# A decoder trunk on one core: first norm's squares on VectorE, more places for split weights and score blocks

## The chip, the cores and the metric

The kernel runs on one core of a Trainium2 chip. The core has TensorE (PE, matrix products; a row "PEld" is its weight load), VectorE (DVE), ScalarE (ACT) and GpSimd (POOL), which run side by side, each in the order of its own instruction list, and SyncE (SP), which issues most DMA transfers. SBUF is the on-chip memory that the engines work in, PSUM the banks that PE adds into, DRAM the chip's large memory. The metric is the time of one execution on the device in microseconds, less is better. An instruction starts when those ahead of it in its engine's list have started and the data and places that it needs are there.

## What is computed

Two decoder layers on 1024 tokens of width 1024, float32. Layer 0 mixes tokens by retention heads and RWKV-7 heads, layer 1 by attention over a window of 128 tokens with a learned sink for each head; each is followed by a dense SwiGLU network.

```python
for layer in range(2):
    n = rms_norm(h, norm1_g[layer])
    h = h + (retention_rwkv_mixer(n, ...) if layer == 0 else swa_sink_mixer(n, ...))
    n = rms_norm(h, norm2_g[layer])
    h = h + (silu(n @ w_gate) * (n @ w_up)) @ w_down
return rms_norm(h, final_g)

# swa_sink_mixer, a block of 128 queries against 256 keys
s = where(valid, q @ k.T / 8, -inf)
m = maximum(s.max(-1), sink)
e = exp(s - m)
o = (e / (e.sum(-1) + exp(sink - m))) @ v
```

## The kernel before

Activations lie transposed, 128 channels on the partitions and tokens along the row, in two halves of 512 tokens (hf 0 and 1). A float32 product is made of three products in a faster type: every operand is split into a high part (a cast on ACT) and a low part (value minus high part), and `gemm` (L327) adds hi x hi, hi x lo and lo x hi for each of eight blocks of 128 channels, 24 matmuls of 128x512 for one column of weights.

**Split weights.** `wraw` (L288) loads a raw column into one of two "wr" places. `wsplit` (L310) casts it in two pieces on ACT (L318) and subtracts on POOL (L319), into tiles from `wtile` (L305): a ring of four "w" places, two for a column, or, while `w6` is set, of six that take in the two "wr" places too. In layer 0's input projection the first half's split columns are also written to DRAM (`keep`, L321), and the second half loads them back with `wkept` (L295). `Plan` (L105) orders that layer when the program is built: it holds the projection columns as jobs (`prefetch`, L135, loads the next two), and advances generators such as `first_norm` (L495) by due times. After that the tile framework's scheduler sets the final order of each engine's list from its own model of time, so an edit moves more than the lines it touches.

**First norm.** `loads` (L471) issues x and the first two weight columns. `first_norm` multiplies each of eight blocks of x by the norm's gain and splits it (`gained`, L444, L449 on ACT and L450 on DVE), squares it on ACT (L505), and has PE sum each square over the channels by a product with a matrix of ones: eight products into one PSUM tile. `factor` (L455) then takes the logarithm (L459) and the exponential (L460) for the inverse root rs, and POOL multiplies it into the rotary cos and sin (L464). The evacuation of a projection multiplies by rs, so PE starts with projections before rs is known. rs also goes into `second_norm` for the second half.

**Around the second layer** (from L1690 on): `down` and `rest_d` (L1447) finish layer 0's network, `rest_d(0)` for the first half, `rest_d(1)` for the second; a column of the latter is split ahead. `attn` (L1472) does the first half's attention while two columns' worth and more of `rest_d(1)` remain as fill; `form0` (L1103) normalises the first half for the next network, block by block: product with the norm (`normed`, L1099, on DVE into one of four "u0" places), a write to DRAM, and `split` (L337), whose cast is on ACT (L339) and whose low part (L341) alternates between POOL and DVE. `ffn_early` (L1216) does first products of the network. In layer 1 `form0` and the early columns stand beside the second half's attention.

**Attention.** For each of four groups of heads two q columns are projected (`proj`, L1479, evacuation L1483 and L1484), then four blocks of 128 queries follow: scores on PE (L1526), mask added on DVE into a tile "s" (L1530), maximum on DVE (L1536), exponentials on ACT (L1543), scaling on DVE (L1549), transposes on PE (L1556) into PSUM, copies into "pT" (L1558 on ACT, L1560 on DVE), products with v on PE (L1566), split of the result (L1572 on ACT, L1573 on DVE). There are two "s" places, three of the small "st4" and two "pT", and the tiles that hold v before its transposes (L1507) use the "s" places as well.

## Time and profile before

| | us |
|---|---|
| median of 3 runs | 2442.09 (2437.88 to 2443.95) |
| profiled execution, its own time | 2449.47 |
| its span, first to last instruction | 2447.7 |
| mean granted clock of PE | 0.981 |

Times of a row in the timeline are microseconds from the start of the span: start, duration, engine, line, operation, output <- inputs, shape, how many alike are put together (x4); in square brackets how long the engine stood idle before it and which engine and tile released it. In a table of stretches a row gives the stretch, its length, then for each engine its busy time and instruction count, the granted clock, the DMA engines' busy share and GB/s. One float32 product with the ones matrix shows as two records.

### The profile page before, as it was taken

The numbers are of one execution on the slowest core, as the hardware profiler recorded it, in microseconds if no ns is written. First come the engines' busy times: TensorE is split into PE (matmuls) and PEld (weight loads), VectorE is DVE, ScalarE is ACT, GpSimd is POOL, SyncE is SP. The second block draws the span as 40 slices with busy tenths as digits, with TensorE's granted clock in tenths as the row PEclk, the third lists the DMA queues.
The fourth block names the chain that finished last, engine by engine and source line by source line (L and its number), as shares of the span: only waits on it lengthen the run. The fifth ranks groups of instructions, "written<-read, shape, count | busy, mean of one in ns | idle before, by whom it ended". The sixth has DMA issues, their size and how long they took to land.

```text
span 2447.7 us, 35747 instructions
## 1 busy us (share of the span) xinstructions
PE 2358.9 (96%) x13112; PEld 1850.2 (76%) x13112; DVE 1624.3 (66%) x2463; ACT 1036.2 (42%) x1907; POOL 1204.8 (49%) x977
## 2 busy tenths in 40 slices
PE   8899999989999999999999999899999999999997
PEld 6677777777777888787778777677687788887786
DVE  4766755775466557887675348547727788787766
ACT  5344443223555433333333545445635333333336
POOL 6455332221453047676576433252241677777665
PEclk9999999999999999999999999899999999999999
DMA  7554553433344645553564222131235556546653
GB/s 279 195 197 175 178 172 118 148 113 119 129 161 157 212 152 209 205 203 132 192 254 156 97 78 69 36 135 61 91 127 196 185 195 218 216 180 247 230 206 108
DMA packets 168750, 399.60 MB, mean 163 GB/s; under 512 B 43008, under 2 KB 45696, under 8 KB 168576
## 3 DMA queue, kind: packets, MB, share of 16 engines
q1 hardware_dynamic: 165456, 391.82, 45.7%
q10 hardware_dynamic: 2832, 4.45, 0.5%
q8 instruction: 104, 1.70, 0.3%
q0 software_dynamic: 288, 1.05, 0.1%
q14 instruction: 70, 0.57, 0.1%
HBM read 271.81 MB, written 120.06 MB: 160 GB/s over the span
## 4 chain that ended last, share of the span: by engine, by line
PE 61%; DVE 7%; DMA 4%; ACT 3%; issue 2%; POOL 1%; SPq 0%; DVEq 0%; ACTq 0%; POOLq 0%
PE ps_m L1151 7%; PE ps_m L1153 6%; PE ps_m L1152 6%; PE ps_f L333 5%; PE ps_f L334 5%; PE ps_f L335 5%; PE ps_f L1151 3%; PE ps_f L1152 3%; PE ps_f L1153 3%; PE ps_m L232 2%; PE ps_r L1151 2%; PE ps_c L1153 2%; PE ps_c L1151 2%; PE ps_c L1152 2%; PE ps_r L1153 2%
## 5 line engine op out<-in xcount | busy, mean ns | idle before, releaser
L319 POOL TENSOR_TENSOR w<-wr,w 128x512 fp32r<-128x512 f32 x228 | 301.5, 1327 | 558.3 <-ACT w L318 551.4
L232 PE MATMUL ps_f<-n,w 128*128 128x512 f32 x1440 | 389.7, 418 | 3.2 <-DVE n L450 2.0
L232 PEld LDWEIGHTS ps_f<-n,w 128*128 128x128 f32 x1440 | 271.7, 194 | 88.7 <-issue 25.2
L318 ACT CAST w<-wr 128x512 fp32r<-128x512 f32 (+1 forms) x276 | 167.3, 612 | 237.8 <-PE ps_f L335 130.1
L333 PE MATMUL ps_f<-n,w 128*128 128x512 f32 x472 | 191.8, 408 | 6.4 <-ACT n L339 3.4
L334 PE MATMUL ps_f<-n,w 128*128 128x512 f32 x472 | 191.3, 405 | 0.4 <-POOL n L341 0.4
L335 PE MATMUL ps_f<-n,w 128*128 128x512 f32 x472 | 188.7, 401 | 0.3 <-POOL w L319 0.3
L319 POOL TENSOR_TENSOR w<-wq,w 128x512 fp32r<-128x512 f32 x90 | 129.9, 1452 | 33.0 <-ACT w L318 32.9
L1151 PE MATMUL ps_f<-n,w 128*128 128x512 f32 x349 | 139.0, 398 | 5.1 <-ACT u L1302 2.5
L1153 PE MATMUL ps_f<-n,w 128*128 128x512 f32 x349 | 137.6, 394 | 1.3 <-POOL w L1325 1.3
L1152 PE MATMUL ps_f<-n,w 128*128 128x512 f32 x349 | 137.5, 394 | 0.0
L1158 DVE TENSOR_TENSOR nq<-ps_m,u 128x512 f32<-128x512 f32 x88 | 58.7, 685 | 108.4 <-PE ps_m L1153 108.3
L1151 PE MATMUL ps_m<-n,w 128*128 128x512 f32 x293 | 115.0, 392 | 1.2 <-DVE sg L1202 0.6
L1153 PE MATMUL ps_m<-n,w 128*128 128x512 f32 x293 | 114.9, 393 | 0.9 <-POOL w L1325 0.9
L1152 PE MATMUL ps_m<-n,w 128*128 128x512 f32 x293 | 114.8, 392 | 0.0
L333 PEld LDWEIGHTS ps_f<-n,w 128*128 128x128 f32 x472 | 91.3, 194 | 29.7 <-ACT n L339 3.7
L341 POOL TENSOR_TENSOR n<-nq,n 128x512 fp32r<-128x512 f32 x64 | 104.8, 1648 | 10.6 <-ACT n L339 10.6
L334 PEld LDWEIGHTS ps_f<-n,w 128*128 128x128 f32 x472 | 91.0, 193 | 24.6 <-issue 4.8
L335 PEld LDWEIGHTS ps_f<-n,w 128*128 128x128 f32 x472 | 90.7, 192 | 21.9 <-issue 2.1
L1325 POOL TENSOR_TENSOR w<-wd,w 128x512 fp32r<-128x512 f32 (+1 forms) x53 | 75.6, 1432 | 49.3 <-ACT w L1324 47.8
L1153 PE MATMUL ps_m<-cb,w 128*128 128x512 f32 x232 | 91.6, 395 | 0.0
L1151 PE MATMUL ps_m<-cb,w 128*128 128x512 f32 x232 | 91.6, 395 | 0.0
(510 smaller groups left out, 6216.6 us busy)
## 6 DMA issues: line engine op xcount, KB each, us to landing
hc<-n SPq DMA_DIRECT2D x74, 512.0 KB, 2.6
wsp<-w SPq DMA_DIRECT2D x60, 512.0 KB, 3.1
w<-wsp SPq DMA_DIRECT2D x60, 512.0 KB, 3.7
wq<-in_w_gate SPq DMA_DIRECT2D x44, 512.0 KB, 4.1
u<-u SPq DMA_DIRECT2D x88, 256.0 KB, 2.9
n<-hc SPq DMA_DIRECT2D x43, 512.0 KB, 5.6
hid<-n SPq DMA_DIRECT2D x66, 256.0 KB, 2.0
ha<-hc SPq DMA_DIRECT2D x33, 512.0 KB, 6.5
```

Source lines behind the costliest of these rows:

```text
L232: self.nc.tensor.matmul(out, lhsT, rhs, **kw)
L318: nc.scalar.copy(hi[:, :n], raw[:, c])
L319: self.lo.tensor_tensor(out=lo[:, :n], in0=raw[:, c], in1=hi.bitcast(F32)[:, :n], op=ALU.subtract)
L333: nc.tensor.matmul(ps, hi, rh, start=k == 0, stop=False)
L334: nc.tensor.matmul(ps, hi, rl, start=False, stop=False)
L335: nc.tensor.matmul(ps, lo, rh, start=False, stop=k == n - 1)
L341: e.tensor_tensor(out=lo, in0=src, in1=hi.bitcast(F32), op=ALU.subtract)
L1151: mm(ps, hi, xh, start=first and k == 0, stop=False, skip_group_check=True)
L1152: mm(ps, hi, xl, start=False, stop=False, skip_group_check=True)
L1153: mm(ps, lo, xh, start=False, stop=last and k == len(w) - 1, skip_group_check=True)
L1158: add = lambda o, x, y: V.tensor_tensor(out=o, in0=x, in1=y, op=ALU.add)
L1325: nc.gpsimd.tensor_tensor(out=lo, in0=v, in1=hi.bitcast(F32), op=ALU.subtract)
```

## The change

The edits are these:

- First norm: the eight squares are added on DVE into one tile, and one ones-product takes the place of eight. The generator gives way once with a due time of 3.0 ahead of it. A small activation at the program's start goes ahead of the first real one on ACT.
- The first three projection columns are split in `loads` or right after, are not written to DRAM, and the second half loads and splits them again (`twice`).
- `K.wx` gives other places for split weights: six places "wd1" while `rest_d(0)` runs, and two more ("wx", six in all) during the attention stage. `nw` now advances always, so which place a later stage starts at is another.
- Two columns of `rest_d(1)` are split ahead instead of one, and before the pools of the attention open.
- Attention: three "s" places, four "st4", three "pT".
- `form0`: all low parts on DVE.

```diff
--- before.py
+++ after.py
@@ -108,7 +108,7 @@
 
     def __init__(self, K):
         self.K, self.now, self.ev, self.banks = K, 0.0, {}, []
-        self.gens, self.jobs, self.cur, self.ahead = [], deque(), None, 0
+        self.gens, self.jobs, self.cur, self.twice = [], deque(), None, ()
 
     def chain(self, g):
         self.gens.append([g, (), self.now])
@@ -134,11 +134,15 @@
 
     def prefetch(self):
         for i, j in enumerate(list(self.jobs)[:2]):
-            if j["raw"] is None and j["hf"] == 0:
+            twice = j["col"] in self.twice
+            if j["raw"] is None and (j["hf"] == 0 or twice):
                 j["raw"] = self.K.wraw(self.K.A["w_in"][j["col"]])
             if i == 0 and j["hl"] is None:
                 kept = self.K.wsp[j["col"]]
-                j["hl"] = self.K.wkept(kept) if j["hf"] else self.K.wsplit(j["raw"], keep=kept)
+                if twice:
+                    j["hl"] = self.K.wsplit(j["raw"])
+                else:
+                    j["hl"] = self.K.wkept(kept) if j["hf"] else self.K.wsplit(j["raw"], keep=kept)
 
     def busy(self):
 
@@ -206,13 +210,16 @@
         self.dr = ctx.enter_context(tc.tile_pool(name="dr", bufs=2, space=bass.MemoryType.DRAM))
         self.n = 0
         pad = ctx.enter_context(tc.tile_pool(name="pad", bufs=1, side="right"))
-        nc.gpsimd.memset(pad.tile([P, 120], F32, tag="pad", name="pad"), 0.0)
+        pt = pad.tile([P, 120], F32, tag="pad", name="pad")
+        nc.gpsimd.memset(pt, 0.0)
+        nc.scalar.activation(pt[:, :16], pt[:, :16], AF.Copy)
         self.pv = self.t(self.pp, [P, NPV], "pv")
         nc.scalar.dma_start(self.pv, A["pvec"])
         self.cst = {}
         for nm in ("ones", "eps"):
             self.cst[nm] = self.const(self.pp, nm)
         self.h, self.plan = [None, None], None
+        self.wx = None
         self.w6, self.nw, self.owed, self.lo = False, 0, [], self.nc.gpsimd
         self.hid = [self.dram(f"hid{i}", [FT, P, HT]) for i in range(4)]
         self.hc = [self.dram(f"hc{L}", [NP, 4, P, 2, HT]) for L in range(2)]
@@ -304,7 +311,12 @@
 
     def wtile(self):
 
-        i = self.nw = (self.nw + 1) % 6 if self.w6 else 0
+        pool, tag, n, only = self.wx or (None, "", 0, False)
+        if only:
+            return self.t(pool, [P, 2, HT], tag, n, F32R)
+        i = self.nw = (self.nw + 1) % (6 if self.w6 else 4 + n)
+        if i >= 4 and n:
+            return self.t(pool, [P, 2, HT], tag, n, F32R)
         return self.t(self.pp, [P, 2, HT], *(("w", 4) if i < 4 else ("wr", 2)), F32R)
 
     def wsplit(self, raw, width=1024, keep=None):
@@ -472,17 +484,24 @@
 
         nc, mp, rp = self.nc, self.mp, self.rp
         x0 = []
+        first = [self.plan.jobs[i] for i in range(3)]
+
+        self.plan.twice = [j["col"] for j in first]
         for k in range(KT):
             x = self.t(rp, [P, HT], "r2", 8)
             self.keep(nc.sync.dma_start(x, self.A["xT"][k, :, 0:HT]))
             x0.append(x)
             if k == 0:
-                raw = self.plan.jobs[0]["raw"] = self.t(self.pp, [P, 1024], "wr", 2)
+                raw = self.t(self.pp, [P, 1024], "wr", 2)
                 for o in (0, HT):
-                    self.keep(nc.sync.dma_start(raw[:, o : o + HT], self.A["w_in"][self.plan.jobs[0]["col"]][:, o : o + HT]))
+                    self.keep(nc.sync.dma_start(raw[:, o : o + HT], self.A["w_in"][first[0]["col"]][:, o : o + HT]))
+                first[0]["hl"] = self.wsplit(raw)
             if k == 4:
-                raw = self.plan.jobs[1]["raw"] = self.t(self.pp, [P, 1024], "wr", 2)
-                self.keep(nc.sync.dma_start(raw, self.A["w_in"][self.plan.jobs[1]["col"]]))
+                raw = self.t(self.pp, [P, 1024], "wr", 2)
+                self.keep(nc.sync.dma_start(raw, self.A["w_in"][first[1]["col"]]))
+                first[1]["hl"] = self.wsplit(raw)
+        raw = first[2]["raw"] = self.t(self.pp, [P, 1024], "wr", 2)
+        self.keep(nc.sync.dma_start(raw, self.A["w_in"][first[2]["col"]]))
         wua = self.t(mp, [P, 512], "wua")
         self.keep(nc.sync.dma_start(wua[0:64, :], self.A["w_up"]))
         self.keep(nc.sync.dma_start(wua[64:128, :], self.A["a_up"]))
@@ -497,18 +516,17 @@
         nc = self.nc
         x0 = self.loads()
         n8 = self.n8(self.pp)
-        self.nT = []
-        ps = self.pst("m", [P, HT])
+        self.nT = [self.gained(x0[k], "n1a", n8, k) for k in range(KT)]
+        self.plan.done("n0")
         for k in range(KT):
-            self.nT.append(self.gained(x0[k], "n1a", n8, k))
             sq = self.t(self.pp, [P, HT], "nq", 4)
             nc.scalar.activation(sq, x0[k], AF.Square)
-            if k == 0:
-                self.plan.done("n0")
-                yield (), 0.0
-            self.mm(ps, self.cst["ones"], sq, start=k == 0, stop=k == KT - 1)
-            if k < KT - 1:
-                yield (), 0.5
+            if k:
+                nc.vector.tensor_tensor(out=sq, in0=acc, in1=sq, op=ALU.add)
+            acc = sq
+        yield (), 3.0
+        ps = self.pst("m", [P, HT])
+        self.mm(ps, self.cst["ones"], acc, start=True, stop=True)
         self.factor(0, ps)
 
     def second_norm(self):
@@ -1108,7 +1126,7 @@
                 f = self.t(sp, [P, HT], "u0", 4)
                 self.normed(f, 0, kk, g, r)
                 self.nc.sync.dma_start(self.bd[kk], f)
-                self.split(f, *self.X[nm][k], k % 2 == 0)
+                self.split(f, *self.X[nm][k], False)
 
     def form1(self, g, r, n8, cb, ft):
 
@@ -1498,7 +1516,7 @@
         vt = self.t(ap, [P, 5, 256], "vt", 2)
         if hf:
             G.tensor_copy(vt[:, 0, :], self.pvt[:, 4, :])
-        vcs = [self.t(ap, [P, HT], "s", 2) for _ in range(2)]
+        vcs = [self.t(ap, [P, HT], "s", 3) for _ in range(2)]
         for i, vc in enumerate(vcs):
             proj(10 + i, vc, bias=self.col("bqkv", 10 + i))
         for i, vc in enumerate(vcs):
@@ -1517,7 +1535,7 @@
                 k0 = 1 if (hf == 0 and b == 0) else 0
                 kw = slice(P * k0, 256)
                 nk = 256 - P * k0
-                s = self.t(ap, [P, 4, 256], "s", 2)
+                s = self.t(ap, [P, 4, 256], "s", 3)
                 for e in range(2):
                     ps = self.pst("rc"[e], [P, 2, 256])
                     a = slice(64 * e, 64 * e + 64)
@@ -1531,7 +1549,7 @@
                         out=s.rearrange("p (i e) k -> p e i k", e=2)[:, e, :, kw], in0=ps[:, :, kw],
                         in1=amask[:, kw].rearrange("p (o t) -> p o t", o=1).to_broadcast([P, 2, nk]), op=ALU.add,
                     )
-                st4 = self.t(ap, [P, 4, 4], "st4", 3)
+                st4 = self.t(ap, [P, 4, 4], "st4", 4)
                 m, den, es = st4[:, 0, :], st4[:, 1, :], st4[:, 2, :]
                 V.tensor_reduce(out=m, in_=s[:, :, kw], axis=AX.X, op=ALU.max)
                 sk = sink[:, 4 * g : 4 * g + 4]
@@ -1549,7 +1567,7 @@
                     V.tensor_scalar(
                         out=s[:, h, kw], in0=s[:, h, kw], scalar1=den[:, h : h + 1], scalar2=None, op0=ALU.mult
                     )
-                pT = self.t(ap, [P, 2, 4, P], "pT", 2)
+                pT = self.t(ap, [P, 2, 4, P], "pT", 3)
                 for kb in range(k0, 2):
                     pt = self.pst("m", [P, 4, P])
                     for h in range(4):
@@ -1701,12 +1719,15 @@
         X = [K.rest_x(0, fp, fz)]
         raws = [K.rest_w(0, d, fp) for d in range(4)]
         X.append(K.rest_x(1))
+        K.wx = fp, "wd1", 6, True
         run(K.rest_d(0, X[0], fp, raws))
+        K.wx = None
+        ws = [K.wsplit(K.rest_w(1, d), len(X[1]) * P) for d in range(2)]
         close(gz, gf)
         g1, nB = K.pool("nB", "right")
         ga, ap = K.pool("at", "right")
         K.attn_open(ap)
-        ws = [K.wsplit(K.rest_w(1, 0), len(X[1]) * P)]
+        K.wx = ap, "wx", 2, False
         n0 = K.norm(K.kt(K.h[0]), "n1b", K.n8(nB), ap)
         f = K.rest_d(1, X[1], stop=2, ws=ws)
         next(f)
@@ -1722,6 +1743,7 @@
         K.w_o(1, c1)
         r = K.factor_of(1, sp)
         early(1, sp, 5, 6)
+        K.wx = None
         close(ga)
         gc, cb = K.pool("cb", "right")
         gt, ft = K.pool("ft", "left")
```

Line numbers in the rows below are those of each kernel: L333, L334, L335 (gemm), L341, L1099, L1483, L1526, L1556 and L1566 of before are L345, L346, L347, L353, L1117, L1501, L1544, L1574 and L1584 of the changed kernel, and L232 is L239.

The first place is PE's list from the program's start. ps_f tiles are projections, n the split x, w split weights, ps_m with c_ones the product with ones. Before:

```order
L232 MATMUL ps_m_153<-nq_156,c_ones_67 128x512
L232 MATMUL ps_f_185<-n_28_145,w_167 128x512
L232 MATMUL ps_f_185<-n_32_149,w_167 128x512
L232 MATMUL ps_f_185<-n_28_145,w_167 128x512 x2
L232 MATMUL ps_m_153<-nq_191,c_ones_67 128x512
L232 MATMUL ps_f_185<-n_32_149,w_167 128x512
L232 MATMUL ps_f_185<-n_28_145,w_167 128x512
L232 MATMUL ps_f_185<-n_29_146,w_167 128x512
L232 MATMUL ps_m_153<-nq_199,c_ones_67 128x512
L232 MATMUL ps_f_185<-n_33_150,w_167 128x512
```

and in the changed kernel, rows 39 to 48 of PE's list:

```order
L239 MATMUL ps_f_315<-n_33_160,w_263 128x512
L239 MATMUL ps_f_315<-n_37_164,w_263 128x512
L239 MATMUL ps_f_219<-n_40_167,w_114 128x512
L239 MATMUL ps_f_219<-n_36_163,w_114 128x512
L239 MATMUL ps_f_271<-n_40_167,w_130 128x512
L239 MATMUL ps_f_271<-n_36_163,w_130 128x512
L239 MATMUL ps_m_235<-nq_204,c_ones_68 128x512
L239 MATMUL ps_f_315<-n_33_160,w_263 128x512 x2
L239 MATMUL ps_f_315<-n_37_164,w_263 128x512
L239 MATMUL ps_f_315<-n_33_160,w_263 128x512
```

Before, a ones-product stands in the first row, and the other seven among the first projections; now there is one, behind 44 rows of projections (the first two and the beginning of the third job).

The second place is PE's list at the end of the first half's attention, from the last scores (ps_r, ps_c <- q) on. Before:

```order
L334 MATMUL ps_f_13626<-n_1867_12193,w_13623 128x512
L335 MATMUL ps_f_13626<-n_1863_12189,w_13623 128x512
L1566 MATMUL ps_y_13188<-pT_13181,vt_12273 64x256 x2
L1526 MATMUL ps_r_13284<-ks_1880_12270,q_1895_12359 128x256 x2
L1526 MATMUL ps_c_13288<-kc_1875_12234,q_1895_12359 128x256 x2
L1556 MATMUL ps_m_13219<-c_ident_135,s_13193 128x128
L1556 MATMUL ps_m_13225<-c_ident_135,s_13193 128x128
```

Only transposes and products with v follow until the attention ends. In the changed kernel, a few rows behind its last scores:

```order
L1584 MATMUL ps_y_13045<-pT_13032,vt_12284 64x256 x4
L1574 MATMUL ps_m_13275<-c_ident_150,s_13249 128x128 x4
L1574 MATMUL ps_m_13281<-c_ident_150,s_13249 128x128 x4
L1584 MATMUL ps_y_13090<-pT_13077,vt_12284 64x256 x4
L345 MATMUL ps_f_13569<-n_1868_12200,w_13566 128x512
L345 MATMUL ps_f_13603<-n_1868_12200,wx_13600 128x512
L345 MATMUL ps_f_13637<-n_1868_12200,w_13634 128x512
L1584 MATMUL ps_y_13199<-pT_13192,vt_12284 64x256 x2
L346 MATMUL ps_f_13569<-n_1872_12204,w_13566 128x512
L347 MATMUL ps_f_13569<-n_1868_12200,w_13566 128x512
```

Products of another stage (L345 to L347) now stand behind the last scores, 27 in all up to the end of the attention; two runs of transposes and products with v remain with none among them.

The third place is DVE's list where `form0` of layer 1 meets the first rows of the second half's attention: L1099 makes u, L341 is a low part on DVE, L1483 evacuates k or v columns. Before:

```order
L1099 SCALAR_TENSOR_TENSOR u_2149_13878<-h_962_6507,pv_65,rs_13825 128x512
L1483 TENSOR_TENSOR kc_2168_13951<-ps_f_13960,rs_13520 128x512
L341 TENSOR_TENSOR n_2142_13859<-u_2148_13873,n_2138_13855 128x512
L1099 SCALAR_TENSOR_TENSOR u_2150_13883<-h_961_6506,pv_65,rs_13825 128x512
L341 TENSOR_TENSOR n_2144_13861<-u_2149_13878,n_2140_13857 128x512
L1099 SCALAR_TENSOR_TENSOR u_2151_13888<-h_962_6507,pv_65,rs_13825 128x512
L1099 SCALAR_TENSOR_TENSOR u_2152_13893<-h_961_6506,pv_65,rs_13825 128x512
L1099 SCALAR_TENSOR_TENSOR u_2153_13898<-h_962_6507,pv_65,rs_13825 128x512
L341 TENSOR_TENSOR n_2143_13860<-u_2152_13893,n_2139_13856 128x512
L1483 TENSOR_TENSOR s_13993<-ps_f_14003,rs_13520 128x512
L341 TENSOR_TENSOR n_2145_13862<-u_2153_13898,n_2141_13858 128x512
L1483 TENSOR_TENSOR s_13994<-ps_f_14038,rs_13520 128x512
```

and in the changed kernel:

```order
L353 TENSOR_TENSOR n_2147_13870<-u_2151_13874,n_2143_13866 128x512
L353 TENSOR_TENSOR n_2149_13872<-u_2152_13879,n_2145_13868 128x512
L1501 TENSOR_TENSOR kc_2173_13962<-ps_f_13971,rs_13531 128x512
L353 TENSOR_TENSOR n_2147_13870<-u_2153_13884,n_2143_13866 128x512
L1117 SCALAR_TENSOR_TENSOR u_2155_13894<-h_966_6517,pv_66,rs_13836 128x512
L353 TENSOR_TENSOR n_2149_13872<-u_2154_13889,n_2145_13868 128x512
L1117 SCALAR_TENSOR_TENSOR u_2156_13899<-h_967_6518,pv_66,rs_13836 128x512
L1117 SCALAR_TENSOR_TENSOR u_2157_13904<-h_966_6517,pv_66,rs_13836 128x512
L1117 SCALAR_TENSOR_TENSOR u_2158_13909<-h_967_6518,pv_66,rs_13836 128x512
L353 TENSOR_TENSOR n_2148_13871<-u_2155_13894,n_2144_13867 128x512
L1501 TENSOR_TENSOR s_14004<-ps_f_14014,rs_13531 128x512
```

Five low parts stand on DVE ahead of the first evacuation of v (L1501 s), where three stood, and three behind it, where one stood; POOL's list holds none of them any more.

## Prediction

> **What bounds the kernel now.** I read the page first, for which engine is full; then a table of stretches, to find where PE is not full; then the timeline around each hole, for what ended the wait there.
>
> ```profile
> PE 2358.9 (96%) x13112; PEld 1850.2 (76%) x13112; DVE 1624.3 (66%) x2463; ACT 1036.2 (42%) x1907; POOL 1204.8 (49%) x977
> PE 61%; DVE 7%; DMA 4%; ACT 3%; issue 2%; POOL 1%; SPq 0%; DVEq 0%; ACTq 0%; POOLq 0%
> ```
>
> PE is busy 96% of the span and holds 61% of the chain that ended last. So an edit pays only if it removes PE work or one of PE's holes. The stretches that the change touches (busy time and instruction count per engine, then granted clock, DMA share, GB/s):
>
> ```profile
> 0.00:33.00 33.00, 26.32 (x91) 18.09 (x92) 9.49 (x13) 18.62 (x29) 16.44 (x27) 1.00 0.88 295
> 300.00:325.00 25.00, 22.81 (x128) 16.35 (x128) 19.44 (x38) 8.79 (x15) 8.76 (x10) 0.86 0.90 277
> 1440.00:1527.00 87.00, 86.97 (x454) 62.98 (x452) 71.07 (x163) 50.29 (x146) 26.66 (x24) 1.00 0.18 58
> 1527.00:1569.00 42.00, 33.03 (x161) 21.86 (x162) 27.12 (x76) 18.32 (x60) 1.91 (x2) 0.84 0.03 13
> 1440.00:1569.00 129.00, 120.00 (x615) 84.84 (x614) 98.19 (x238) 68.62 (x206) 28.57 (x25) 0.95 0.13 44
> 1634.00:1760.00 126.00, 125.03 (x653) 90.19 (x652) 89.21 (x204) 74.39 (x203) 35.32 (x27) 1.00 0.20 72
> ```
>
> Attention of the first token half (1440 to 1569) keeps PE full for 87 us, then loses 42.00 - 33.03 = 8.97 us in its last 42. Attention of the second half (1634 to 1760) loses 0.97. Starts and seams of stages make up the rest.
>
> **First norm (A).**
>
> ```profile
> 18.21 1.02 PE L232 MATMUL ps_m<-nq,c_ones 128*128 128x512 f32 x2
> 18.66 1.49 PE L232 MATMUL ps_f<-n,w 128*128 128x512 f32 x4
> 19.99 1.02 PE L232 MATMUL ps_m<-nq,c_ones 128*128 128x512 f32 x2
> 22.13 0.69 ACT L459 ACTIVATE rs<-ps_m,c_eps 128x512 f32<-128x512 f32 x1 [4.49 <-PE ps_m L232]
> 27.14 0.63 ACT L460 ACTIVATE rs<-rs 128x512 f32<-128x512 f32 x1
> 27.89 1.31 POOL L464 TENSOR_TENSOR c_cos<-c_cos,rs 128x512 f32<-128x512 f32 x1
> 31.52 3.00 POOL L319 TENSOR_TENSOR w<-wr,w 128x512 fp32r<-128x512 f32 x2
> 32.87 1.43 PE L232 MATMUL ps_f<-n,w 128*128 128x512 f32 x5 [0.30 <-POOL w L319]
> ```
>
> One ones-matmul (two records, x2) with four projection matmuls takes 19.99 - 18.21 = 1.78 us. Four projections at 0.23 (such matmuls start 0.22 to 0.23 apart, as at 1547.10 and 1547.32 below) are 0.91, so a ones-matmul costs 0.87, and seven removed are 6.1 us of PE. That is the most A can give. But the fourth projection job starts at 32.87 on a low part that stands on POOL behind the cos and sin products, and those wait for rs, ready at 27.14 + 0.63 = 27.77. So the gain is how much earlier rs comes. In the new order the single ones-matmul stands behind 44 projections, and ACT has the third column's casts ahead of the logarithm; behind the logarithm stay a table load and the second activation. I place rs between 22.5 (PE alone decides, 6.1 us off and a little more) and 27 (it waits for loads: the DMA share here is 0.88), and take 25.0. The fourth job then starts near 30.0: **-2.9 us (-1 to -6.1)**. The seven adds on VectorE lie under the loads of x. The six dropped copies to DRAM, 512 KB each, relieve the DMA queues.
>
> **Second token half's start (B).**
>
> ```profile
> 308.62 1.65 PE L232 MATMUL ps_f<-n,w 128*128 128x512 f32 x3 [1.71 <-DVE n L450]
> ```
>
> PE waits here for normalised x, in a stretch with DMA share 0.90. Each of the three columns now brings 512 KB raw instead of 1 MB of split parts, and x stands ahead of them. Against it stand six casts on ACT and six low parts on POOL that were loaded before. The idle in this stretch is 25 - 22.81 = 2.2 us: **-1 (-3 to +2)**, the upper end being two low parts (1.5 each, half of the 3.00 above) left in the open and 1 us regained.
>
> **form0, both layers (C, E).** All eight low parts go to VectorE.
>
> ```profile
> 726.99 0.67 DVE L570 TENSOR_TENSOR h<-h,ps_f 128x512 f32<-128x512 f32 x1
> 727.81 0.76 PE L333 MATMUL ps_f<-n,w 128*128 128x512 f32 x1 [3.35 <-ACT n L339]
> ...
> 1610.75 5.88 DVE L1099 SCALAR_TENSOR_TENSOR u<-h,pv,rs 128x512 f32<-128x512 f32 x4 [4.79 <-ACT rs L358]
> ...
> 1618.92 0.68 DVE L341 TENSOR_TENSOR n<-u,n 128x512 fp32r<-128x512 f32 x1
> ...
> 1623.59 1.75 DVE L341 TENSOR_TENSOR n<-u,n 128x512 fp32r<-128x512 f32 x1
> ...
> 1625.27 0.68 DVE L1483 TENSOR_TENSOR s<-ps_f,rs 128x512 f32<-128x512 f32 x1
> ```
> ```profile
> 1623.08 1.72 POOL L341 TENSOR_TENSOR n<-u,n 128x512 fp32r<-128x512 f32 x1
> ```
> ```profile
> 1547.10 0.39 PE L334 MATMUL ps_f<-n,w 128*128 128x512 f32 x1
> 1547.32 0.40 PE L335 MATMUL ps_f<-n,w 128*128 128x512 f32 x1
> ...
> 1626.75 1.12 PE L1507 MATMUL ps_m<-c_ident,s 128*128 128x128 f32 x4 [2.85 <-ACT s L1484]
> 1628.10 0.63 PE L335 MATMUL ps_f<-n,w 128*128 128x512 f32 x1
> 1628.52 0.63 PE L333 MATMUL ps_f<-n,w 128*128 128x512 f32 x1
> ...
> 1631.93 0.53 PE L335 MATMUL ps_f<-n,w 128*128 128x512 f32 x1
> ```
>
> A low part on VectorE takes 0.68 alone and 1.75 beside POOL's own low part: 1.07 more. In layer 1, PE's transposes of v (1626.75) wait for the bias on the s tile, and that for VectorE's L1483 at 1625.27, which stands behind form0's work. Ahead of it VectorE has 12 instructions before and 14 after, while POOL's operations beside them fall from 8 to 4 (only weight splits stay). By these rows that is 12 x 0.68 + 8 x 1.07 = 16.7 us before (the trace has 1625.27 - 1610.75 = 14.5) and 14 x 0.68 + 4 x 1.07 = 13.8 after. I take 2 us earlier. The hole of 2.85 shrinks to under 1, and with it goes most of what follows it: matmuls 0.42 apart (1628.10, 1628.52) where others are 0.22 apart (1547.10, 1547.32), nine of them up to 1631.93, 9 x 0.2 = 1.8 us or a little more. **E: -3.5 (-4.8 to 0).** In layer 0 the hole of 3.35 ends at 727.81, just behind a residual add that stood on VectorE between form0's instructions (726.99). Four more operations come ahead of such adds (4 x 0.68 = 2.7), and four waits for POOL go (up to 4 x 1.07 = 4.3): **C: -0.5 (-1.5 to +1.5)**, near the difference.
>
> [...]
>
> **Seam to the second half's rest (D1).** Two weight columns are now split ahead instead of one.
>
> ```profile
> 1383.07 0.79 PE L333 MATMUL ps_f<-n,w 128*128 128x512 f32 x1 [2.56 <-ACT w L318]
> 1384.09 1.91 PE L356 MATMUL ps_y<-nq,c_ones 128*128 128x512 f32 x2
> 1386.57 0.39 PE L335 MATMUL ps_f<-n,w 128*128 128x512 f32 x1
> ```
>
> From 1383.07 to 1386.57 PE runs four products and one ones-matmul, 4 x 0.22 + 0.87 = 1.75 at full rate, in 3.50: 1.75 lost beside the hole of 2.56, 4.3 together. With the splits done, 34 products instead of 2 stand ahead of the norm's ones. ACT and POOL must do the second column's casts and subtractions while the first half's rest still runs; the six added places let them. **-3.5 (-4.3 to -1).**
>
> **Attention, first half (D2).**
>
> ```profile
> 1540.00:1550.00 10.00, 10.00 (x36) 6.57 (x32) 6.22 (x22) 2.55 (x10) 0.00 (x0) 0.66 0.00 0
> ```
> ```profile
> 1551.17 1.09 PE L1556 MATMUL ps_m<-c_ident,s 128*128 128x128 f32 x8
> 1553.75 1.09 PE L1566 MATMUL ps_y<-pT,vt 128*64 128x256 f32 x8 [1.49 <-ACT pT L1558]
> 1556.31 1.14 PE L1556 MATMUL ps_m<-c_ident,s 128*128 128x128 f32 x8 [1.48 <-DVE s L1549]
> 1559.37 1.09 PE L1566 MATMUL ps_y<-pT,vt 128*64 128x256 f32 x8 [1.92 <-ACT pT L1558]
> 1565.93 1.60 PE L333 MATMUL ps_f<-n,w 128*128 128x512 f32 x3 [0.46 <-ACT n L1572]
> ```
>
> Between 1549 and 1566 PE has only attention's own steps, and every one waits for a DVE or ACT step of the same block: the projection work that fills such waits is used up. Recoverable are the 8.97 us idle and what matmuls lost at a lower clock: 1540 to 1550 PE is busy all through at a granted 0.66, some 3.4 us lost, and a little more from 1567 on, 3.6 by estimate: 12.6 in all. The two more weight places and the third s and pT places spread the fill between the blocks, and 27 products (27 x 0.22 = 6 us) now stand behind the last scores, a third s place letting scores be written while two older blocks are in softmax and transposes. The last blocks still end with chains of 5.1 us each (1551.17 to 1556.31) that only partly overlap, so I leave some 4.5 us idle: **-8 (-12.6 to 0)**. VectorE does not forbid it: 98.19 us of work in a stretch that would be 129 - 12.6 = 116 long. It is the next bound.
>
> **The rest (F).** Attention of the second half has 0.97 to gain; its early FFN columns can stand further ahead; elsewhere split places are only renamed: **-0.6 (-2 to +3)**.
>
> **Sum:** -2.9 - 1 - 0.5 - 3.5 - 3.5 - 8 - 0.6 = -20.0 us. The profiled execution took 2449.47 us (span 2447.7), so 2429.5 for one like it; that execution lies 7.4 above the median of 2442.09, from which the forecast is **2422**.
>
> **Rivals.**
> 1. *The attention tail stays bound by latency.* The blocks without fill are each waited for by the chain of scores, softmax, transposes; if the scheduler's spread leaves the last two bare, D2 gives 0: 2422 + 8 = **2430**. For it: behind the last scores the new order still has a run of transposes and pT.v steps with no product among them. Chance 0.17.
> 2. *PE is all that bounds the start.* A in full (-6.1) and B at -3: 2422 - 3.2 - 2 = **2417**. For it PE's 26.32 of 33 and the 4.49 us that ACT waited for PE; against it the 3.75 us from rs (27.77) to the low part (31.52), which do not shrink with PE's work. Chance 0.13.
> 3. *VectorE and POOL lock each other at the start.* If each of six low parts on POOL holds up an add by 1.07 us, the adds end up to 6.4 us later, rs at 28.5 instead of 25.0: A is +0.7, sum -16.4: **2426**. Chance 0.12. [...]
> 4. *The third s place turns on VectorE.* VectorE runs in order. If the mask adds of block n+2 come ahead of the scales of block n, PE's transposes come late in every block; this decides once VectorE's spare time, 129 - 98 = 31 us in the first half and 126 - 89 = 37 in the second, is used up. Each attention then loses another 12.6, as the first loses now: -20 + 8 + 12.6 + 12.6 = +13.2, **2455**, slower than before. The order keeps most scales first. Chance 0.04.
> 5. *The holes only move.* PE's waits come back at the next seam (x loads, writes of u, the last blocks), and only A's and D1's halves stay: -4, **2438**. Chance 0.12.
>
> **How the numbers follow.** The forecast (2412 to 2430) has the remaining 0.42. Cases 1, 2 and 3 also end faster by over 0.3% (7.3 us, about what a measurement of this kernel can tell from no change): 0.42 + 0.17 + 0.13 + 0.12 = 0.84. Case 5 is within it, 0.12; case 4 is slower, 0.04. The low end takes A, D1, E and half of what D2 has left to give: 2422 - 3.2 - 0.8 - 1.3 - 2.3 - 2 (B) = 2412, less 2 for F: 2410. The high end takes cases 1 and 3 together, 2434, and the near half of case 5: 2437. Some 0.1 lies outside on either side together with case 4.
>
> **What would show it.** Right: no hole over 1 us with ACT or DVE as releaser between 1549 and 1566 of before's program place; the hole at the transposes of v below 1 us and no matmuls 0.42 apart after it; the hole at the seam gone; rs near 25 and the fourth job near 30. Wrong: PE's transposes waiting for L1549's successor throughout both attentions (case 4); a fourth job near 27 or near 33 (cases 2, 3); DVE's form0 work still ending 14.5 us after it began.

## The result and the profile after

| | us |
|---|---|
| before, median of 4 | 2441.06 (2437.88 to 2443.95) |
| changed, median of 4 | 2421.15 (2416.25 to 2422.73) |
| ratio, 95% interval | 0.9911 (0.9893 to 0.9929) |
| changed, span of its profile | 2420.2 |

The forecast was 2422. The sum was right; several of its terms were not. The two profiles are 27.5 us apart, the medians 19.9: the profiled execution of before (2449.47) was a slow one of a kernel whose executions range over almost 18 us (2431.03 to 2448.68 in 31 others). Where that spread comes from is part of what follows.

The page of the changed kernel, engines:

```profile
PE 2338.5 (97%) x13098; PEld 1838.3 (76%) x13098; DVE 1635.1 (68%) x2478; ACT 1035.8 (43%) x1914; POOL 1204.0 (50%) x975
```

The seam, the first attention, form0 of layer 1 and the second attention, as stretches of the changed kernel (length, then busy time and count of PE, PEld, DVE, ACT, POOL, then granted clock):

```profile
1362.00:1374.00 12.00, 12.00 (x55) 9.94 (x54) 6.83 (x11) 5.88 (x10) 3.73 (x3) 1.00 0.05 12
1422.00:1509.00 87.00, 87.00 (x465) 62.83 (x465) 79.44 (x183) 51.30 (x161) 25.36 (x22) 1.00 0.17 52
1509.00:1545.50 36.50, 30.95 (x154) 19.93 (x151) 22.48 (x57) 15.99 (x47) 3.85 (x3) 0.95 0.09 29
1587.00:1610.00 23.00, 23.00 (x106) 18.90 (x105) 16.90 (x20) 13.18 (x23) 13.58 (x9) 1.00 0.57 194
1604.30:1774.00 169.70, 167.81 (x850) 121.56 (x848) 107.36 (x240) 94.60 (x249) 50.77 (x39) 1.00 0.25 86
```

The same stretches of before that were not shown:

```profile
1378.00:1390.00 12.00, 9.44 (x34) 6.68 (x33) 3.42 (x6) 7.83 (x12) 4.22 (x5) 0.86 0.30 97
1611.00:1634.00 23.00, 19.88 (x78) 15.76 (x77) 16.62 (x15) 10.89 (x19) 16.87 (x11) 0.85 0.55 186
1634.00:1800.00 166.00, 165.03 (x850) 120.28 (x849) 105.21 (x240) 93.44 (x247) 49.44 (x38) 1.00 0.26 91
```

At the seam and at form0 PE is now full (12.00 of 12, 23.00 of 23). The first attention's tail still idles 36.50 - 30.95 = 5.55 us of the 8.97. The last row of each fence is the surprise: the same stretch of program, 850 records in both traces, is 3.7 us **longer** after the change, and most of that, 167.81 - 165.03 = 2.8, is busy time, not waiting.

### The profile page after: what moved, and what is told of

The parts are those of the page before. It is cut to its first block, busy times and chain, and to the rows that moved or that the text cites. A ratio compares the mean times of both kernels' runs of the same rounds, so it can differ in the third digit from the quotient of the medians.

```text
span 2420.2 us, 35718 instructions
## 1 busy us (share of the span) xinstructions
PE 2338.5 (97%) x13098; PEld 1838.3 (76%) x13098; DVE 1635.1 (68%) x2478; ACT 1035.8 (43%) x1914; POOL 1204.0 (50%) x975
## 5 line engine op out<-in xcount | busy, mean ns | idle before, releaser
L331 POOL TENSOR_TENSOR w<-wr,w 128x512 fp32r<-128x512 f32 x196 | 264.6, 1355 | 450.3 <-ACT w L330 391.5
L239 PE MATMUL ps_f<-n,w 128*128 128x512 f32 x1440 | 386.6, 417 | 13.5 <-ACT w L330 5.7
L239 PEld LDWEIGHTS ps_f<-n,w 128*128 128x128 f32 x1440 | 270.5, 193 | 97.3 <-issue 23.0
L330 ACT CAST w<-wr 128x512 fp32r<-128x512 f32 x244 | 148.0, 612 | 185.5 <-PE ps_f L347 77.5
L345 PE MATMUL ps_f<-n,w 128*128 128x512 f32 x356 | 142.2, 399 | 3.5 <-ACT n L351 2.6
L346 PE MATMUL ps_f<-n,w 128*128 128x512 f32 x356 | 142.9, 401 | 0.0
L347 PE MATMUL ps_f<-n,w 128*128 128x512 f32 x356 | 141.7, 398 | 0.0
L1169 PE MATMUL ps_f<-n,w 128*128 128x512 f32 x322 | 127.2, 396 | 4.1 <-DVE h L1369 1.8
L1170 PE MATMUL ps_f<-n,w 128*128 128x512 f32 x322 | 126.4, 392 | 0.0
L1171 PE MATMUL ps_f<-n,w 128*128 128x512 f32 x322 | 125.8, 391 | 0.0
L353 POOL TENSOR_TENSOR n<-nq,n 128x512 fp32r<-128x512 f32 x64 | 106.1, 1670 | 10.9 <-ACT n L351 10.9
L1171 PE MATMUL ps_m<-n,w 128*128 128x512 f32 x282 | 110.3, 391 | 0.0
L1170 PE MATMUL ps_m<-n,w 128*128 128x512 f32 x282 | 110.3, 391 | 0.0
L1169 PE MATMUL ps_m<-n,w 128*128 128x512 f32 x282 | 109.8, 390 | 0.0
L331 POOL TENSOR_TENSOR wx<-wr,wx 128x512 fp32r<-128x512 f32 (+1 forms) x38 | 49.3, 1299 | 105.0 <-ACT wx L330 105.0
L1169 PE MATMUL ps_m<-cb,w 128*128 128x512 f32 x240 | 94.8, 395 | 0.8 <-ACT w L330 0.8
L1171 PE MATMUL ps_m<-cb,w 128*128 128x512 f32 x240 | 94.8, 395 | 0.0
L1170 PE MATMUL ps_m<-cb,w 128*128 128x512 f32 x240 | 94.7, 395 | 0.0
L345 PEld LDWEIGHTS ps_f<-n,w 128*128 128x128 f32 x356 | 67.4, 189 | 21.7 <-ACT n L351 3.0
```

Of the source, the lines that this page charges most:

```text
L239: self.nc.tensor.matmul(out, lhsT, rhs, **kw)
L330: nc.scalar.copy(hi[:, :n], raw[:, c])
L331: self.lo.tensor_tensor(out=lo[:, :n], in0=raw[:, c], in1=hi.bitcast(F32)[:, :n], op=ALU.subtract)
L345: nc.tensor.matmul(ps, hi, rh, start=k == 0, stop=False)
L346: nc.tensor.matmul(ps, hi, rl, start=False, stop=False)
L347: nc.tensor.matmul(ps, lo, rh, start=False, stop=k == n - 1)
```

## The experiments

Twelve runs followed: each part of the change alone and two halves of one part, the whole again, the whole less one part, and three new kernels, one of them twice. Beside the times I read stages: the start of the same TensorE instruction in two traces, and from that how much longer or shorter a stretch was than in the first profile of before (us; one execution each). The stretches are named by before's times.

| kernel | time ratio (95%) | 0 to 660 | seam 1345 to 1395 | attention 1, 1430 to 1575 | form0, 1600 to 1655 | attention 2, 1655 to 1800 |
|---|---|---|---|---|---|---|
| norm part alone | 0.9971 (0.9957 to 0.9986) | -8.9 | 0.0 | +0.1 | -2.5 | 0.0 |
| form0 alone | 0.9992 (0.9977 to 1.0007) | -3.7 | 0.0 | -2.5 | -6.0 | 0.0 |
| places alone | 1.0014 (0.9997 to 1.0031) | -4.5 | +0.2 | -3.3 | +0.1 | +2.4 |
| weights alone | 0.9962 (0.9944 to 0.9980) | -2.9 | -3.9 | -1.2 | -0.9 | -1.6 |
| squares only | 0.9973 (0.9958 to 0.9987) | -7.2 | -1.6 | -2.2 | -1.0 | -0.1 |
| loads only | 0.9995 (0.9978 to 1.0011) | -4.0 | 0.0 | +0.2 | -2.6 | -0.1 |
| changed, first profile | 0.9911 (0.9893 to 0.9929) | -9.4 | -4.5 | -6.2 | -5.9 | +3.7 |
| changed, again | 0.9924 (0.9901 to 0.9947) | -9.3 | -4.5 | -3.7 | -5.8 | +3.6 |
| changed, old places | 0.9901 (0.9878 to 0.9924) | -5.6 | -4.5 | -3.7 | -5.9 | -1.6 |
| new places in attention 1 only | 0.9873 (0.9846 to 0.9900) | -14.6 | -4.5 | -4.0 | -5.8 | -1.6 |
| the same again | 0.9884 (0.9862 to 0.9906) | -10.4 | -4.5 | -8.0 | -5.8 | -1.6 |
| changed, scores in turn | 0.9899 (0.9875 to 0.9924) | -12.2 | -4.5 | -8.2 | -5.8 | +0.9 |
| attention 1 only, scores in turn | 0.9881 (0.9857 to 0.9906) | -11.1 | -4.5 | -7.7 | -5.8 | -1.6 |

Read the columns first. Attention 2 repeats within 0.2 us wherever the same code stands there, and with all of the new code so do the seam and form0; before's code spreads there too (squares only has it at the seam and shows -1.6, loads only has it in form0 and shows -2.6). The columns 0 to 660 and attention 1 do not repeat: kernels with before's own code in 0 to 660 show 0, -3.7, -4.5 and -2.9, and the changed code of attention 1 shows anything from -3.7 to -8.0. A single profile can't price those two.

**Each part alone.** The edits are the parts of the change; the norm part is everything in `Plan`, `loads`, `first_norm` and the pad tile, "weights" everything with `wx`, `wtile` and `ws`:

```diff
-                self.split(f, *self.X[nm][k], k % 2 == 0)
+                self.split(f, *self.X[nm][k], False)
```
```diff
-                s = self.t(ap, [P, 4, 256], "s", 2)
+                s = self.t(ap, [P, 4, 256], "s", 3)
...
-                pT = self.t(ap, [P, 2, 4, P], "pT", 2)
+                pT = self.t(ap, [P, 2, 4, P], "pT", 3)
```

> The kernel before with the first-norm part alone (squares added on VectorE, first three columns split in the load and again for the second half). Theory (parts stand at their own places): the fourth projection job starts near 30.6 us, as in the changed kernel, instead of 32.87, and by 600 us of the span the program is 5 to 6 us ahead of before, as the changed kernel is (5.6); nothing more is gained behind it, so the time is about 0.3% less (-4 to -8 us). Rival (the start's gain is eaten by waits in the mixer; the 5.6 belongs to the one profiled execution of before): 0 to -3 us.

Medians of 2433.69 against 2441.13: -7.4 us, the theory's upper end. The fourth job started at 31.17.

> The kernel before with form0's low parts all on VectorE, nothing else. Theory: in layer 1 the hole of 2.85 us ahead of the transposes of v and the matmuls 0.43 apart behind it go (-4 to -5 us there), layer 0's form0 gives -0.5 to -1: in all -4 to -6 us. Rival (that hole went because other weight places and split columns brought the projections of v earlier, not because of VectorE): the hole stays over 2 us and the time moves by less than 2 us.

The theory held at its place, -6.0 us; the whole kernel's -0.08% is within its interval of no change, so the gain stands shown by the stage, not by the time.

> The kernel before with three score, four statistic and three pT places, nothing else. Theory (fill and places are both needed): the first attention's tail still has no products behind the last scores, and half of the 6 us comes: -2 to -4 us; the second attention loses about 2 us. Rival A (places alone do it): -6 us or more in the first attention. Rival B (weights alone do it): 0 in the first attention, and with the second attention's loss the kernel is 2 us slower.

The two stages came as the theory had them, -3.3 in attention 1 and +2.4 in attention 2, but the first is one profile of a column that does not repeat. By time nothing is gained (+0.14%, within noise of none; 2.5 us slower by medians, which is rival B's number). And the tail does have products behind the last scores here, ten from 1535.58 to 1537.78, which the theory denied.

> The kernel before with the added weight places and the two columns split ahead, nothing else. Theory: the hole of 2.56 us at the seam and the slow matmuls behind it go (-4.6 us), and the first attention gains the other half of its 6 us (-2 to -4): in all -6 to -9 us. Rival A of the places: -4 to -5 us only, all at the seam. Rival B: -10 us or more.

-6.4 us by medians: the theory's lower end. The seam gave -3.9, attention 1 only -1.2, and attention 2 -1.6, which nobody had expected.

**Taking the norm part in two.** Squares only leaves `Plan` and `loads` as before; loads only leaves `first_norm` as before.

> The kernel before with the squares added on VectorE and one ones-product (and the small activation ahead), but with the first three columns kept in DRAM as before. Theory (the fourth job waits for the cos and sin products and a third column's casts, so both the earlier rs and the earlier loads are needed): fourth job near 32 us, and 2 to 4 us less in all. Rival A (the ones-products were the whole cost of the start): fourth job near 30.6 to 31.2 as in the changed kernel, and 6 to 8 us less in all, as the first-norm part together. Rival B (the loads do it): no difference, fourth job near 33.

> The kernel before with the first three columns split early, not written to DRAM and split again in the second half, but eight ones-products as before. Theory: fourth job near 32 us, 2 to 4 us less in all. Rival A of the squares: no difference. Rival B: 6 to 8 us less. In any case the second half's start (300 to 320 us) shows whether the six casts and low parts there cost or save: between -1 and +2 us.

The squares carry it by time: 2434.7 (-6.4) alone, 2440.34 (-0.7) for the loads, as rival A had it; the theory's 2 to 4 us from each is out, though the fourth job of loads only did start at 32.10. But rival A's mechanism fell with its own number: in squares only, TensorE stood 3.23 and 1.51 us for casts of weights around 26 and 28 us, so the start got later, not earlier. By 83 us the program was some 1.5 us **behind** before; it was 3.5 ahead at 133 us. What differs between is the clock. This stretch, in the trace of before, of form0 alone, of loads only and of the changed kernel:

```profile
100.00:124.00 24.00, 21.91 (x190) 17.07 (x189) 18.94 (x48) 5.57 (x10) 6.86 (x8) 0.93 0.48 163
```
```profile
100.00:124.00 24.00, 23.17 (x214) 17.99 (x213) 19.72 (x52) 6.49 (x12) 7.41 (x8) 1.00 0.43 141
```
```profile
100.00:124.00 24.00, 20.18 (x179) 15.60 (x178) 17.80 (x47) 5.30 (x11) 7.59 (x8) 0.86 0.44 146
```
```profile
96.00:120.00 24.00, 23.70 (x234) 18.77 (x233) 19.88 (x50) 6.51 (x12) 7.58 (x10) 1.00 0.54 168
```

Of the five kernels with eight ones-products the granted clock here is 0.93, 1.00, 0.86, 0.86 and 0.86; the nine traces with squares on VectorE all have 1.00. Before and form0 alone have the same instructions here in the same order, and differ by a fall of the clock. From 95 to 125 us the nine gained some 3 us more than the five, so a good part of the squares' gain is likely that the clock no longer falls there. Why it does not is open. In before, places alone and weights alone TensorE idles 1.4 and 0.7 us just ahead of the fall, in loads only 3.8; in form0 alone, without a fall, 0.8; in eight of the nine 0.3 to 0.5. But the ninth (new places in attention 1 only, its second profile) idles 1.2 and 0.9 and keeps its clock, and no run set the length of these holes alone. The second half's start, 260 to 342 us, moved by 0.1 us with the loads alone.

**The whole again, and less one part.**

> The changed kernel once more, for a second profile and more times beside the three below. Theory (the program gains about 20 us, and several us of any one profile come from the clock in the mixer, which falls behind a hole in some executions and not in others): ratio 0.990 to 0.993; the seam, the first attention and form0 of layer 1 gain the same as in its first profile within 0.5 us each, the stretch from 45 to 660 us differs by some us. Rival (every stage repeats): all stages within 0.5 us.

The ratio, the seam and form0 came as the theory had them. Attention 1 did not repeat (-6.2, then -3.7), and 0 to 660 did (-9.4, then -9.3), though the clock fell at other places in it: the theory had it the other way round for these two.

> The changed kernel with the score, statistic and pT places as before (2, 3, 2). Theory: the third places are worth 3 to 5 us in the first attention and cost 2.5 to 3.7 us in the second, so their net is small: within 2 us of the changed kernel. Rival (the places carry the first attention): 5 to 6 us slower than the changed kernel.

Neither. Without the third places the kernel is not within 2 us of the changed one but 6.3 faster by medians (2416.44 against 2422.7); the intervals of the two ratios overlap. Attention 2 is 5.3 shorter (-1.6 against +3.7).

**Where attention 2 loses.** The next kernel keeps the third places for the first half's attention, and holds one score and one pT place with a dummy tile during the second's (the four "st4" places stay):

```diff
+        held = []
+        if hf:
+            for tag, sh in (("s", [P, 4, 256]), ("pT", [P, 2, 4, P])):
+                d = self.t(ap, sh, tag, 3)
...
+                G.memset(d, 0.0)
+                held.append(d)
```

> The changed kernel, where the second half's attention is left with two score and two pT places (one of each is held by a dummy tile). Theory: the first attention as in the changed kernel; in the second, the same 850 or so TensorE records take 165 us of busy time again instead of 167.8, and idle falls from 1.9 to 1 us: 2.5 to 3.7 us faster than the changed kernel. Rival (the loss there comes from the weight places or from where the stage starts): no difference.

> The kernel with third score and pT places in the first attention alone, once more, for more times. Theory (5.3 us of its gain over the changed kernel are the second attention, the rest came from executions in which the clock fell less often early on): 2414 to 2418 us. Rival (the early gain belongs to this program): 2409 to 2413 us again. In the second attention 164 to 166 us for the same 850 or so TensorE records, as at its first profile (164.4).

Its second attention, from the first of these profiles:

```profile
1599.80:1764.20 164.40, 163.95 (x850) 119.68 (x848) 104.04 (x240) 96.60 (x251) 51.17 (x41) 1.00 0.26 89
```

164.40 us for the 850 records that take 169.70 in the changed kernel: 5.3 us, of which 167.81 - 163.95 = 3.9 is TensorE's busy time. The rival (weight places, or where the stage starts) is out, and the gain is more than the 2.5 to 3.7 that the theory had. The medians are 2410.19 and 2412.92, 8 to 12.5 us under the changed kernel's two (2421.15 and 2422.7), so 3 to 7 us more than this stage explains. The second set came at its rival's number and not at the theory's 2414 to 2418, which speaks for an extra gain of this program. Where it comes from is open: until the second attention TensorE's list is the same as in the changed kernel, the two profiles spread the rest over stretches that do not repeat, and the mean granted clock of the ten executions is hardly higher (0.9886 against 0.9879 in ten of the changed kernel).

The busy time has a cause that the rows show. Two score products of a block, for the tiles ps_r and ps_c, use 64 rows each (the 64 of 64*128), with q and k from partitions 0 to 63 for one tile and 64 to 127 for the other. In before, where they stand next to each other:

```profile
1550.10 0.48 PE L1526 MATMUL ps_r<-ks,q 64*128 64x256 f32 x1
1550.11 0.48 PE L1526 MATMUL ps_c<-kc,q 64*128 64x256 f32 x1
1550.41 0.38 PE L1526 MATMUL ps_r<-ks,q 64*128 64x256 f32 x1
1550.43 0.38 PE L1526 MATMUL ps_c<-kc,q 64*128 64x256 f32 x1
...
1551.17 0.33 PE L1556 MATMUL ps_m<-c_ident,s 128*128 128x128 f32 x1
```

and in the changed kernel's second attention, where the scheduler put other work between:

```profile
1647.53 1.13 PE L1544 MATMUL ps_r<-ks,q 64*128 64x256 f32 x4
1649.95 1.13 PE L1544 MATMUL ps_c<-kc,q 64*128 64x256 f32 x4
```

Next to each other they start 0.01 us apart and eight records (four of them shown) take 1.07 us up to the next product; apart, each four take about as long (1.13), at a granted clock of 1.00 in both places. Pairs that start within 0.06 us of each other: 50 of 64 in before, 42 in the changed kernel, 52 with the old places in this stage. A block has four, so ten pairs are two and a half blocks, by estimate from the 1.07 us some 2.5 of the 3.9 us. TensorE's busy time in the scores alone and in the transposes of a block's weights alone (PE, then PEld) bears this out, first in the changed kernel, then with the old places in this stage:

```profile
1604.30:1774.00 169.70, 24.86 (x128) 14.40 (x128) 1.00 0.25 86
1604.30:1774.00 169.70, 19.86 (x128) 14.63 (x128) 1.00 0.25 86
```
```profile
1599.80:1764.20 164.40, 22.12 (x128) 12.71 (x128) 1.00 0.26 89
1599.80:1764.20 164.40, 18.09 (x128) 14.07 (x128) 1.00 0.26 89
```

The end of a record overlaps the start of the next one (0.39 us long and 0.22 apart at 1547.10 of before), so these differences come out too large together. Counted from start to next start, without idle, the scores lose 2.6 us and the transposes 1.2, while projections and products with v are equal within 0.1. The transposes are parted too: TensorE changes between kinds of product 100 times in the changed kernel and 84 times with the old places. That this is their cost is argued, not tested.

**Scores in turn.** I tried to get the pairs by writing the products r, c, r, c:

```diff
-                for e in range(2):
-                    ps = self.pst("rc"[e], [P, 2, 256])
...
+                pss = [self.pst(t, [P, 2, 256]) for t in "rc"]
+                for i in range(2):
+                    for e in range(2):
```

> The changed kernel with the four score products of a block written in turn for the two PSUM tiles (r, c, r, c) instead of two and two. Theory (two score products on different 64 rows of the array run at the same time when they stand next to each other; apart, each takes its full time): the share of score records that start within 0.06 us of one for the other tile rises from 82 of 248, and TensorE's busy time in the two attentions falls by 1 to 2 us each: 2 to 4 us faster than the changed kernel. Rival (both PSUM tiles must now be free at the same time, and mask adds come later): the pairs come, but idle grows as much, no gain or a loss.

> The same with the score products written in turn too. Theory (what writing in turn gave came from the order that the scheduler then found in both attentions, not from pairs; with two places in the second half that stage is already without idle): the first attention as in the kernel with scores in turn (4 us less than the changed kernel), the second between 164 and 167: 2412 to 2417 us. Rival (more splitting of the scores, 57 rows of scores in the second half where 39 stand, loses the pairs): fewer than 45 paired score records in the second half, over 166 us there, and 2417 us or more.

The first kernel's theory failed in its mechanism: 48 and 42 pairs in the two attentions against 44 and 42 in the changed kernel, since the scheduler parts them again. It is 6 us faster than the changed kernel by medians (2416.76; the intervals overlap). 2.7 us of that is attention 2, where its order leaves no idle (167.00 of 167.00); the rest lies in the columns that do not repeat. With the places in attention 1 only it gave 2412.13, as the second theory had it and the same as without writing in turn. The second attention stands at -1.6 as there, with 56 pairs, so the rival's loss of pairs did not come either.

## Why the prediction was right, step by step

All the signs that were named for being right came: rs and the fourth job, no hole over 1 us in the first attention's tail, no hole and no slow matmuls at the transposes of v, no hole at the seam. The sizes are another matter. To price a term I take the mean of the profiles with the new code at that place less the mean of those with the old.

- **A and B, forecast -2.9 and -1: about -7.** The path was read rightly. rs is ready at 24.97 + 0.63 = 25.60 (forecast 25.0, before 27.77), and the fourth job starts at 30.63 (forecast 30.0), held, as forecast, by POOL's chain behind rs and not by TensorE:

```profile
22.97 0.69 ACT L471 ACTIVATE rs<-ps_m,c_eps 128x512 f32<-128x512 f32 x1 [3.89 <-PE ps_m L239]
23.68 1.28 ACT L472 ACT_TABLE_LOAD   x1
24.97 0.63 ACT L472 ACTIVATE rs<-rs 128x512 f32<-128x512 f32 x1
25.68 1.29 POOL L476 TENSOR_TENSOR c_cos<-c_cos,rs 128x512 f32<-128x512 f32 x1 [5.48 <-ACT rs L472]
...
30.63 2.60 PE L239 MATMUL ps_f<-n,w 128*128 128x512 f32 x10 [2.22 <-POOL w L331]
```

  That is 2.2 us, and in all eight traces with the whole norm part this matmul starts between 30.6 and 31.2. But in most of them the gain does not last: TensorE now waits some 2 us there, where it waited 0.30, and in five of the eight the granted clock falls to half right behind that hole (in the second profile of the changed kernel it is 0.50 from 31.3 to 34.5). By 36 us these five are ahead by 0.1 to 0.7 us, the other three by 1.8 to 2.2. The rest of -7 comes later, which the sum did not have: some 3 with the clock at 100 to 120 us, and 2 at 625 to 660 us, where the clock fell in before (0.86 from 625 to 650), in form0 alone and in the changed kernel with old places, but in none of the other eleven traces. No edit touches that stretch, so these 2 us are luck. B itself gave nothing: the hole of 1.71 at the second half's start is there as 1.63 and 1.95.

```profile
301.57 0.96 PE L239 MATMUL ps_f<-n,w 128*128 128x512 f32 x3 [1.63 <-DVE n L462]
304.49 2.80 PE L239 MATMUL ps_f<-n,w 128*128 128x512 f32 x7 [1.95 <-DVE n L462]
```

- **E, forecast -3.5: -4.7** (-5.9 against the first profile of before). VectorE reaches the first v evacuation 1598.51 - 1586.93 = 11.6 us after form0 begins, 14.5 before: 2.9 earlier, what the two prices (0.68 and 1.07) gave by the formula, 16.7 - 13.8 (each side is 2.2 above its trace, and the difference holds); taking 2 was too careful. The hole is gone wholly.

```profile
1586.93 3.78 DVE L1117 SCALAR_TENSOR_TENSOR u<-h,pv,rs 128x512 f32<-128x512 f32 x4 [4.73 <-ACT rs L370]
...
1594.21 1.79 DVE L353 TENSOR_TENSOR n<-u,n 128x512 fp32r<-128x512 f32 x1
...
1598.51 0.68 DVE L1501 TENSOR_TENSOR s<-ps_f,rs 128x512 f32<-128x512 f32 x1
```

  The low part at 1594.21 still takes 1.79, beside a weight split on POOL (1593.87, 1.59 long), so that price holds in the new kernel too. In layer 0 (C, -0.5) the hole went from 3.35 to 2.57.
- **D1, forecast -3.5: -4.2**, the whole of the 4.3 that was there. It is the added places with the columns split ahead: the weights alone give -3.9, and of the other parts only squares only shows anything there, -1.6 with before's code.
- **D2, forecast -8: -4.6.** This term of the sum was too large. 27 products do stand behind the last scores, but in two pieces: nine up to 1521.8 and 18 from 1531.3 to 1536.3. The steps of the blocks between and behind them have none:

```profile
1523.58 0.66 PE L1574 MATMUL ps_m<-c_ident,s 128*128 128x128 f32 x4 [0.94 <-DVE pT L1578]
1525.19 1.09 PE L1584 MATMUL ps_y<-pT,vt 128*64 128x256 f32 x8 [0.95 <-DVE st L1556]
1527.09 1.80 PE L1574 MATMUL ps_m<-c_ident,s 128*128 128x128 f32 x8 [0.81 <-DVE pT L1578]
...
1531.28 0.50 PE L345 MATMUL ps_f<-n,w 128*128 128x512 f32 x1 [0.48 <-ACT n L1590]
...
1539.32 1.09 PE L1584 MATMUL ps_y<-pT,vt 128*64 128x256 f32 x8 [0.94 <-DVE n L1591]
1541.35 1.09 PE L1584 MATMUL ps_y<-pT,vt 128*64 128x256 f32 x8 [0.94 <-DVE n L1591]
```

  Waits for VectorE and ACT stay in them, seven of 0.5 to 0.95 us and 5.5 in all; the order excerpt had shown such a run without products, and I gave it too little weight. Against before's first profile the weights without the places gave 1.2 and 3.7 in two kernels, the places without the weights 3.3. Part of the 12.6 held recoverable was the clock: attention 1 of before's code was 2.5 shorter in another execution.
- **F, forecast -0.6: about +1** (0 to +2; the stages behind 1800 us do not repeat well enough to say more), two errors inside it. Attention 2 lost 3.7 where 0.97 was thought to be all that could move: rival 4 had the loser's place right and the mechanism wrong, since the cost came as TensorE's own busy time through the order, and not from VectorE running out of room. Against it, 745 to 1345 us, where split places are only renamed, came out some 2 us shorter.

So the errors cancelled: D2 and F gave 5 us less than forecast, A, D1 and E some 5 more. The mechanisms of D1 and E and the path of A were right, D2's in part and F's not; that the sum came within 1 us of the measured median is luck. The rivals: case 1 (D2 gives nothing) is half true; case 2 is out, since the fourth job did not come at 27; case 3 is out as a whole, though two adds did take 1.78 and 1.79 beside POOL (the other five took 0.68); case 5 is out by its time, 2438, though a hole did move to the fourth job.

One premise of E and D1 held in part only: that a hole of 2.5 to 2.9 us brings slow matmuls behind it (1.8 us in E, 1.75 in D1). Norm part alone has the same hole at the transposes of v, 2.85, and no slow matmuls behind it:

```profile
1617.19 0.66 PE L1519 MATMUL ps_m<-c_ident,s 128*128 128x128 f32 x4 [2.85 <-ACT s L1496]
1617.60 0.48 PE L340 MATMUL ps_f<-n,w 128*128 128x512 f32 x1
1617.91 0.40 PE L341 MATMUL ps_f<-n,w 128*128 128x512 f32 x1
1618.15 0.39 PE L339 MATMUL ps_f<-n,w 128*128 128x512 f32 x1
```

A hole of 2.85 us was followed by the fall in one execution and not in the other. In before the clock is 0.50 from 1625.4 to 1632.2, so it fell 1.5 us after the hole began at 1626.75 - 2.85 = 1623.90; in norm part alone the matmuls behind the hole start 0.22 to 0.24 us apart from 1617.91 on, where before's stood 0.42 apart. In the traces of before and of the changed kernel the granted clock is 0.5 or 1.0, and each of the 54 stretches of either (the first and the last of a trace aside) lasts a whole number of 3.41 us; of the 27 at 0.5, 17 lasted 3.41 us, nine 6.83 and one 13.65.

## What to carry to other kernels

A third buffer was not free here even where memory was: it gave the scheduler room to reorder, and the second attention took 3.9 us more of busy time on the very engine that bounds, some 2.5 of them by estimate in score products that no longer ran at the same time. Add it stage by stage, and compare busy time of the same instructions, not idle time alone. Behind holes of 2.56 and 2.85 us on TensorE the clock fell in before, and behind one of 2.85 in norm part alone it did not: price the slow matmuls behind such a hole as a chance, and get several profiles before a gain of under 5 us in such a stretch is believed. The best kernel here takes the change but leaves the second attention its old places: 0.9873 and 0.9884 of before in two sets of runs.

## What the runs showed that I had not expected

- TensorE ran two float32 products of 64 rows each at the same time when their records stood next to each other: they started 0.01 us apart, eight records in 1.07 us, against four in 1.13 where they stood apart.
- The same instructions in the same order ran at a granted clock of 0.93 over 24 us in one execution and of 1.00 in another. Over the 31 executions of before the time falls as the mean granted clock rises: 2431.03 us at 0.989, 2448.68 at 0.983, with a correlation of -0.79 and 1.7 us for each 0.001. So the clock goes with most of their spread. Its mean is 0.9856 in these 31 and 0.9879 in ten executions of the changed kernel; by that slope some 4 of the 20 us gained are clock, an estimate.
